# Weight stream of an S5/GLU/MLP/attention trunk on one core: loads strictly in order of use, the GLU with a third raw buffer, the residual in four loads, the GLU's last k-tiles by token halves, and the first MLP splits queued

## The chip, the cores and the metric

The kernel runs on one core of one Trainium2 chip. The time is the device time of one execution in microseconds (us). The kernel before takes 2044.38 us in the median of 3 runs (2044.13 to 2048.23). The engines are named as the profile names them: PE is TensorE's matmuls, PEld its weight loads, DVE is VectorE, ACT is ScalarE, POOL is GpSimd, SP is SyncE, which issues most DMAs. A q behind a name is the queue of DMA issues and semaphores of that engine.

## The reference

A residual stream `h` of 256 tokens by 2048 features, in fp32, passes through four sub-layers, each with an RMS norm ahead and a residual sum behind. `w_glu_a` and `w_glu_b` are 2048x2048, `w_up` and `w_down` 2048x8192 and back.

```python
def sqrelu_mlp(h, w_up, w_down):
    return jnp.square(jax.nn.relu(h @ w_up)) @ w_down

def s5_mixer(u, ...):          # diagonal complex state space, both directions
    ...
    y = y + d_skip.astype(f32) * uf
    z = jax.nn.gelu(y).astype(u.dtype)
    return (z @ w_glu_a) * jax.nn.sigmoid(z @ w_glu_b)

for i in range(DEPTH):         # DEPTH = 2
    if i % N_MIXERS == 0:
        h = h + s5_mixer(rms_norm(h, s5_norm[j]), ...)
    else:
        h = h + windowed_gqa(rms_norm(h, attn_norm[j]), ...)
    h = h + sqrelu_mlp(rms_norm(h, mlp_norm[i]), mlp_w_up[i], mlp_w_down[i])
```

So the order is S5 with its gated unit (GLU), MLP, windowed attention (32 query heads, 4 key heads, softmax with a sink), MLP.

## The kernel before

**Products.** Tokens lie in two halves of 128 (`tt`). Weights come from memory in fp32 and are split on chip into two parts: `hi`, a copy rounded to the type that TensorE multiplies (ScalarE, L682), and `lo`, raw minus `hi` (VectorE, for some tiles GpSimd, L683). Activations are split in the same way. A product is three matmuls, x_hi·w_hi, x_lo·w_hi and x_hi·w_lo (`mm3`, L721 to L723), of 128 by 128 by 512 each. In the MLP's first product the weights are the stationary operand, 16 k-tiles for each of 64 blocks `fb` (L862 for w_hi with both parts of x, L864 for w_lo).

**Weight stream.** All weights go through one list in the order of their use, `self.wsrc`: first 32 GLU tiles of 128x1024, called `wge` here (512 KB each, loaded from ScalarE's queue), then 16 GLU tiles of 128x2048, `wgl` (1 MB, from SyncE's queue, as all that follow), then the MLP's `wup` and `wdn`, attention's `wqkv` and `wo`, and the second MLP. `wload` takes the next entry, asks for a raw, a `hi` and a `lo` buffer from three rings, issues the DMA and writes the split. `wnext` hands over one split tile and keeps one more loaded ahead. An entry's second field says who subtracts: "v" is VectorE, "g" GpSimd; `WP = range(9, 33)` (L36) names the `wge` entries that go to GpSimd (an entry i is the tile i − 1). `wload_fast` (L686) makes the forms for some `wdn` tiles by further subtractions on VectorE.

**Buffers.** For the 1 MB tiles the ring has two raw buffers (19456 and 21504), three for `hi`, three for `lo`. The MLP adds a raw buffer at 49664 and two at 44032 and 46080, which it gives up at block 45; the space at 49664 is free from the end of S5 on.

**Order.** The code is a program for all engines; a scheduler with a model of their times decides the order of instructions on each engine, and with `tc.issue_after(i)` the code can demand that what follows stands behind instruction `i` on its engine. Each engine then runs its list in order. A DMA issue that waits for its buffer holds back what stands behind it on that queue.

**The stages around the change.** The GLU's sums run for four column blocks `cb` of 512 over 16 k-tiles. Its first 8 k-tiles depend on the first half of S5's output and run while S5's second half is computed (`glu_early`, L792, order 1, 2, 3, 0, mixed with S5's expand products on GpSimd, L564 and L565, and its scan on VectorE, L546 to L548; the scan's states are copied at L622 and used by PE at L650). The other 8 run after S5 (`glu_rest`, L835), and beside each block's matmuls the block before is finished by `glu_post` (L811): partial sums added (L820 for the a side, L821 for the b side), sigmoid, product (L826), residual sum (L827), the norm's multiplication by its gain (L739), and four transposes (L748) into the MLP's input, split at L750 and L751. The last block's `glu_post` is handed to `mlp` as `fin`: there the first two MLP blocks run their first 12 k-tiles, with steps of `fin` between them, then the last 4. The residual is loaded whole (2 MB, L1519) from ScalarE's queue before `glu_rest`. Behind the MLP, attention's output tiles `wo` are split while scores (L1224) and softmax (L1239) run head by head.

**The gate.** In `mlp`, the loads asked for at block 6 (`fb == min(SIX)`, L1022) have their splits queued behind `begin`, which are the ScalarE copy and the VectorE addition of the second block's `up_post` (L869).

## Time and profile before

| | us |
|---|---|
| median of 3 runs | 2044.38 |
| the profiled execution's own time | 2044.0 |
| its span in the trace | 2042.2 |
| PE busy in it | 1979.6 |
| DVE busy | 1632.5 |
| ACT busy | 1140.9 |
| POOL busy | 239.5 |

The mean granted TensorE clock of the profiled execution is 0.995 of full speed. Times in the trace run from the span's start. The stages: S5's first half to about 195 us, the early GLU mixed with S5's second half to 286, the late GLU to 389, the change to the MLP to 408, the first MLP to 1066, attention to about 1290, the second MLP to the end. In rows of groups and of the timeline, "out<-in" are the program's names of buffers, "128x2048" is partitions by elements, x is a count, and a bracket at the end of a row of the timeline holds how long the engine was idle before it and what ended that. A row of waits gives the waiting line, what it waited for, the sum in us, how often, and the longest. "slot" is a piece of the large on-chip buffer, "bank" one of the accumulators of TensorE.

### The profile page before, as it was taken

The page shows a single profiled execution, that of the slowest core. Times are in us where ns is not written, and L with a number is a line of the kernel's source. Part 1 is how long each engine was busy: PE and PEld are TensorE (multiplying, and loading weights), DVE is VectorE, ACT ScalarE, POOL GpSimd, SP SyncE. Part 2 cuts the span into 40 slices and gives each one's busy share as a digit, 9 for nine tenths or more (in the row PEclk, how much of TensorE's full clock was granted, in tenths as well). Part 3 has the DMA queues.
Part 4 walks back from the last instruction along what each step waited for, and adds up shares of the span by engine and source line. Part 5 has one row for each costly group of instructions (what it writes and reads, how often), then busy time and mean ns, then how long its engine had stood idle before and what let it go on. Part 6 is the DMA issues. An engine that isn't in the chain of part 4 may idle for free.

```text
span 2042.2 us, 33455 instructions
## 1 busy us (share of the span) xinstructions
PE 1979.6 (97%) x13646; PEld 1671.3 (82%) x13646; DVE 1632.5 (80%) x2474; ACT 1140.9 (56%) x1404; POOL 239.5 (12%) x210
## 2 busy tenths in 40 slices
PE   4989999999999999999999999999999999999999
PEld 4777777788888888888888876888888888888887
DVE  8889736778888888888887877568788888888885
ACT  5553555455555555665554656555555555565553
POOL 6997830000000000000010000000000000000000
PEclk9999999999999999999999999999999999999999
DMA  3234465555555455675555432555555545576554
GB/s 123 68 97 134 145 243 215 181 185 207 206 188 205 165 204 205 232 253 211 214 179 187 147 133 102 218 182 182 180 212 204 205 165 201 204 277 226 201 195 140
DMA packets 62570, 378.99 MB, mean 186 GB/s; under 512 B 7136, under 2 KB 9472, under 8 KB 20944
## 3 DMA queue, kind: packets, MB, share of 16 engines
q1 hardware_dynamic: 55872, 354.90, 48.8%
q10 hardware_dynamic: 5184, 19.49, 2.9%
q0 software_dynamic: 1360, 2.46, 0.6%
q8 instruction: 107, 1.75, 0.3%
q14 instruction: 47, 0.39, 0.1%
HBM read 372.63 MB, written 2.10 MB: 183 GB/s over the span
## 4 chain that ended last, share of the span: by engine, by line
PE 82%; POOL 6%; DVE 5%; ACT 3%; DMA 2%; issue 1%; ACTq 0%; SPq 0%; POOLq 0%; DVEq 0%
PE bank L953 32%; PE bank L862 23%; PE bank L864 12%; PE bank L721 4%; PE bank L723 4%; PE bank L722 4%; POOL slot L564 2%; DVE slot L683 1%; ACT slot L1239 1%; POOL slot L565 1%; POOL slot L505 1%; DMA slot<-in_wge 1%; PE bank L586 1%; PE bank L650 1%; ACT slot L682 1%
## 5 line engine op out<-in xcount | busy, mean ns | idle before, releaser
L683 DVE TENSOR_TENSOR slot<-slot,slot 128x2048 fp32r<-128x2048 f32 (+1 forms) x277 | 597.4, 2161 | 229.5 <-ACT slot L682 222.6
L682 ACT CAST slot<-slot 128x2048 fp32r<-128x2048 f32 (+1 forms) x301 | 519.7, 1734 | 373.5 <-PE bank L953 96.7
L953 PE MATMUL bank<-slot,slot 128*128 128x512 f32 x2532 | 591.3, 390 | 0.0
L953 PEld LDWEIGHTS bank<-slot,slot 128*128 128x128 f32 x2532 | 472.0, 188 | 95.8
L862 PE MATMUL bank<-slot,slot 128*128 128x512 f32 x2048 | 492.7, 391 | 0.1
L862 PEld LDWEIGHTS bank<-slot,slot 128*128 128x128 f32 x2048 | 380.3, 189 | 75.9 <-DVE ms L759 0.3
L698 DVE TENSOR_TENSOR slot<-slot,slot 128x2048 fp32r<-128x2048 f32 (+2 forms) x132 | 241.2, 1827 | 41.1 <-ACT slot L697 40.3
L864 PEld LDWEIGHTS bank<-slot,slot 128*128 128x128 f32 x2048 | 263.1, 191 | 10.3
L864 PE MATMUL bank<-slot,slot 128*128 128x256 f32 x2048 | 266.3, 283 | 0.0
L697 ACT CAST slot<-slot 128x2048 fp32r<-128x2048 f32 (+2 forms) x132 | 203.2, 1540 | 65.8 <-DVE slot L702 48.1
L721 PE MATMUL bank<-slot,slot 128*128 128x512 f32 x544 | 217.1, 400 | 6.1 <-ACT slot L1264 3.1
L722 PE MATMUL bank<-slot,slot 128*128 128x512 f32 x544 | 213.7, 393 | 0.0
L723 PE MATMUL bank<-slot,slot 128*128 128x512 f32 x544 | 207.8, 395 | 4.7 <-POOL slot L683 4.3
L920 ACT CAST slot<-slot 128x512 fp32r<-128x512 f32 (+2 forms) x188 | 108.1, 593 | 58.2 <-PE bank L953 37.3
L721 PEld LDWEIGHTS bank<-slot,slot 128*128 128x128 f32 x544 | 102.7, 189 | 30.9 <-ACT slot L682 3.7
L723 PEld LDWEIGHTS bank<-slot,slot 128*128 128x128 f32 x544 | 102.1, 189 | 28.5 <-POOL slot L683 5.2
L722 PEld LDWEIGHTS bank<-slot,slot 128*128 128x128 f32 x544 | 102.8, 189 | 21.1 <-issue 1.2
L921 DVE TENSOR_TENSOR slot<-slot,slot 128x512 fp32r<-128x512 f32 (+2 forms) x188 | 118.6, 655 | 0.8 <-ACT slot L920 0.8
L869 ACT COPY slot<-bank 128x256 f32<-128x256 f32 x128 | 47.4, 370 | 121.3 <-PE bank L864 120.7
L994 POOL DMA_DIRECT2D slot<-slot x2 | 1.8, 894 | 899.4 <-ACT slot L993 899.4
L872 ACT ACTIVATE slot<-slot 128x256 f32<-128x256 f32 x128 | 53.1, 416 | 68.8 <-DVE slot L870 68.4
L1149 POOL DMA_DIRECT2D slot<-in_pos x1 | 0.8, 784 | 738.7 <-DVE slot L921 738.7
(243 smaller groups left out, 1896.9 us busy)
## 6 DMA issues: line engine op xcount, KB each, us to landing
slot<-in_wup SPq DMA_DIRECT2D x128, 1024.0 KB, 4.9
slot<-in_wdn SPq DMA_DIRECT2D x128, 1024.0 KB, 5.0
slot<-in_wqkv SPq DMA_DIRECT2D x20, 1024.0 KB, 4.9
slot<-in_wge ACTq DMA_DIRECT2D x32, 512.0 KB, 3.8
slot<-in_wgl SPq DMA_DIRECT2D x16, 1024.0 KB, 5.0
slot<-in_wo SPq DMA_DIRECT2D x16, 1024.0 KB, 4.9
slot<-in_wp SPq DMA_DIRECT2D x12, 1024.0 KB, 5.9
slot<-in_bz SPq DMA_DIRECT2D x16, 336.0 KB, 3.3
```

What stands on the lines that cost most here:

```text
L682: self.nc.scalar.copy(hi[:, c], raw[:, c])
L683: (self.nc.gpsimd if e == "g" else self.nc.vector).tensor_sub(lo[:, c], raw[:, c], hi[:, c].bitcast(F32))
L697: self.nc.scalar.copy(hi, x)
L698: v.tensor_sub(lo, x, hi.bitcast(F32))
L721: pe.matmul(out, lhsT=xh, rhs=wh, start=first, stop=False)
L722: pe.matmul(out, lhsT=xl, rhs=wh, start=False, stop=False)
L723: self.dm = pe.matmul(out, lhsT=xh, rhs=wl, start=False, stop=last)
L862: pe.matmul(bk, lhsT=wh[:, kt], rhs=act[:, kt].rearrange("p x c -> p (x c)"), start=(kt == 0), stop=False)
L864: pe.matmul(bk[:, :L], lhsT=wl[:, kt], rhs=act[:, kt, 0], start=False, stop=(kt == KT - 1))
L920: nc.scalar.copy(o[0], h)
L921: v.tensor_sub(o[1], h, o[0].bitcast(F32))
L953: pe.matmul(bank(bk), lhsT=a[x][:, j], rhs=w[y][:, c], start=bk not in begun, stop=stop and y == 1)
```

## The change

1. A new `fetch` issues every 128x2048 weight load from SyncE's queue behind the one before it, in the order of the list. Before, the scheduler could let one pass another.
2. `WP` begins at 12: the `wge` tiles 8, 9 and 10 have their `lo` made by VectorE and not by GpSimd.
3. The raw buffer at 49664 (`self.raw3`) joins the ring in `glu_rest` behind the first k-tile of block 0, and at the second MLP at its beginning; before, the MLP added it after its first two blocks.
4. The residual is loaded in four pieces of 512 KB, one per `cb`, each behind the last weight cast on ScalarE at that point.
5. In the last `cb`, the last four k-tiles run by token halves (`glu_tail`): 24 matmuls for the first half of the tokens and then 24 for the second. Before, each k-tile ran both halves.
6. In `mlp` the splits of the loads asked for at blocks 2 to 11 are queued behind `begin`; before, only those of block 6.

```diff
-WP = range(9, 33)
+WP = range(12, 33)
...
+    def fetch(self, raw, src):
+        with ExitStack() as order:
+            if self.last is not None:
+                order.enter_context(self.tc.issue_after(self.last.ins))
+            self.last = self.nc.sync.dma_start(raw, src)
...
             raw, hi, lo = (r.next() for r in self.wr)
-            (self.nc.scalar if raw.shape[1] < D else self.nc.sync).dma_start(raw, src)
+            if raw.shape[1] < D:
+                self.nc.scalar.dma_start(raw, src)
+            else:
+                self.fetch(raw, src)
...
-                self.nc.scalar.copy(hi[:, c], raw[:, c])
+                self.cast = self.nc.scalar.copy(hi[:, c], raw[:, c])
...
         raw = self.wr[0].next()
-        self.nc.sync.dma_start(raw, src)
+        self.fetch(raw, src)
...
+    def glu_tail(self, bk, kts):
+        w = []
+        for _ in kts[::2]:
+            w.append([t.rearrange("p (n x c) -> p n x c", n=2, x=2) for t in self.wnext()])
+        for tt in range(2):
+            for i, kt in enumerate(kts):
+                wh, wl = w[i // 2]
+                xh, xl = (self.zk(kt)[:, j, tt * P:(tt + 1) * P] for j in range(2))
+                for x in range(2):
+                    self.mm3(bk[tt][x], xh, xl, wh[:, i % 2, x], wl[:, i % 2, x], False, kt == KT - 1)
             yield
...
-            mm = self.glu_mm(bk, range(8, KT)) if cb else self.mm0
+            mm = self.glu_mm(bk, range(8, KT)) if 0 < cb < 3 else self.mm0
+            if cb == 3:
+                mm = chain(self.glu_mm(bk, range(8, KT - 4), range(8, KT)), self.glu_tail(bk, range(KT - 4, KT)))
+            next(mm)
+            cs = slice(cb * 512, (cb + 1) * 512)
+            with self.tc.issue_after(self.cast.ins):
+                self.nc.scalar.dma_start(self.resid[:, :, cs], self.d["xt"][:, :, cs])
             if post is None:
+                self.raw3 = self.ar.get("wx#49664", [2048], at=49664)
+                self.wr[0].add(self.raw3)
                 drain(mm)
             else:
-                next(mm)
                 interleave(mm, (post, 0.7))
...
+        if self.raw3 is None:
+            self.raw3 = ar.get("wx#49664", [2048], at=49664)
+            self.wr[0].add(self.raw3)
...
-        raw3, raw45 = extra(49664), [extra(at) for at in (44032, 46080)]
-        wraw.add(raw3, *raw45)
+        raw45 = [extra(at) for at in (44032, 46080)]
+        wraw.add(*raw45)
...
-                if fb == min(SIX):
+                if fb < 12:
                     for m in begin:
                         gate.enter_context(self.tc.issue_after(m.ins))
...
-                    wraw.drop(raw3, raw4)
+                    wraw.drop(self.raw3, raw4)
+                    self.raw3 = None
...
-        nc.scalar.dma_start(self.resid, d["xt"])
```

How the order of instructions moves is shown at three places. Line numbers of the changed kernel differ: L683 is L693 there, L678 is L674 for SyncE's loads, L732 L742, L739 L749, L751 L761, L820 and L821 L843 and L844, L826 and L827 L849 and L850, L1224 L1258, L1244 L1278, L1240 and L1241 L1274 and L1275.

The first place is SyncE's queue where the GLU's `wgl` tiles begin. slot_83 is the pair of raw buffers, slot_84 the area of the one at 49664, slot_4752 that of the two at 44032 and 46080, and `in_gains` the norm's gain. Before:

```order
L678 DMA slot_83<-in_wgl 128x2048
L678 DMA slot_84<-in_wup 128x2048
L678 DMA slot_83<-in_wgl 128x2048
L732 DMA slot_77<-in_gains 128x512 x2
L678 DMA slot_4752<-in_wup 128x2048 x2
L678 DMA slot_83<-in_wgl 128x2048 x7
```

The same place in the changed kernel:

```order
L674 DMA slot_83<-in_wgl 128x2048 x2
L742 DMA slot_77<-in_gains 128x512 x2
L674 DMA slot_83<-in_wgl 128x2048
L674 DMA slot_84<-in_wgl 128x2048
L674 DMA slot_83<-in_wgl 128x2048 x2
L674 DMA slot_84<-in_wgl 128x2048
```

Three `wup` loads stood among the GLU's tiles; now none does, and the area of slot_84 takes GLU tiles in turn. The `wup` loads begin behind the last `wgl`.

The second place is VectorE at the end of the GLU's last column block. slot_314 holds the partial sums, slot_77 and slot_73 rows of one token half, slot_4068 and slot_4067 the MLP's input. Before:

```order
L821 TENSOR_TENSOR slot_314<-slot_314,bank 128x512
L751 TENSOR_TENSOR slot_4068<-bank,slot_4068 128x4x128
L820 TENSOR_TENSOR slot_314<-slot_314,bank 128x512
L821 TENSOR_TENSOR slot_314<-slot_314,bank 128x512
L820 TENSOR_TENSOR slot_314<-slot_314,bank 128x512
L683 TENSOR_TENSOR slot_3761<-slot_4752,slot_3761 128x2048
L683 TENSOR_TENSOR slot_2734<-slot_83,slot_4070 128x1024
L826 TENSOR_TENSOR slot_77<-slot_314,slot_77 128x512
L683 TENSOR_TENSOR slot_2735<-slot_83,slot_4070 128x1024
L827 TENSOR_TENSOR slot_73<-slot_73,slot_77 128x512
L826 TENSOR_TENSOR slot_77<-slot_314,slot_77 128x512
L739 TENSOR_TENSOR slot_77<-slot_73,slot_77 128x512
```

In the changed kernel:

```order
L844 TENSOR_TENSOR slot_314<-slot_314,bank 128x512
L843 TENSOR_TENSOR slot_314<-slot_314,bank 128x512
L693 TENSOR_TENSOR slot_2735<-slot_83,slot_4069 128x1024 x2
L844 TENSOR_TENSOR slot_314<-slot_314,bank 128x512
L693 TENSOR_TENSOR slot_2734<-slot_84,slot_4069 128x1024
L843 TENSOR_TENSOR slot_314<-slot_314,bank 128x512
L849 TENSOR_TENSOR slot_77<-slot_314,slot_77 128x512
L693 TENSOR_TENSOR slot_2734<-slot_84,slot_4069 128x1024
L761 TENSOR_TENSOR slot_4067<-bank,slot_4067 128x4x128 x2
L850 TENSOR_TENSOR slot_73<-slot_73,slot_77 128x512
L849 TENSOR_TENSOR slot_77<-slot_314,slot_77 128x512
L749 TENSOR_TENSOR slot_77<-slot_73,slot_77 128x512
```

The second half's b addition (the second L844) stands ahead of the first half's product (the first L849), as the second L821 stood before; the 128x2048 split is gone from between them, and the two L761 of the column block before stand behind that product.

The third place is VectorE in attention, around a split for a `wo` tile (the one into slot_2734). slot_4752 (slot_4755 in the changed kernel) holds small rows of the query norm and masks, slot_6431 (slot_6434) the scores. Before:

```order
L210 TENSOR_TENSOR rs_t<-rs_t,rs_h 128x8
L212 SCALAR_TENSOR_TENSOR slot_4752<-rs_t,slot_4752 128x8
L1191 TENSOR_SCALAR slot_4752<-slot_4752,rstd 128x8
L683 TENSOR_TENSOR slot_2734<-slot_83,slot_4070 128x2048
L1224 ISA slot_6431,mx<-bank,slot_4752 128x256
```

In the changed kernel this split stands here:

```order
L1274 TENSOR_TENSOR den<-den,es 128x4
L1275 RECIPROCAL den<-den 128x4
L1278 TENSOR_SCALAR slot_6434<-slot_6434,den 128x256 x4
L1299 TENSOR_TENSOR slot_9576<-bank,slot_9576 128x4x128
L693 TENSOR_TENSOR slot_2734<-slot_83,slot_4069 128x2048
L1221 TENSOR_REDUCE hms<-slot_8091 128x8
```

The split moved from ahead of the head group's scores to behind the end of its softmax (and one of the two splits that came before it moved up to the scores). No line of the diff names attention; this is the scheduler's answer to the rest.

More of the change, by code (lines that the diff above doesn't have):

```diff
@@ L2 @@
 from contextlib import ExitStack
+from itertools import chain
 import numpy as np
@@ L774, in zk, with glu_mm @@
         return self.z[kt // 8][:, KQ[kt // 8][(kt % 8) // 2], kt % 2]
-    def glu_mm(self, bk, kts):
+    def glu_mm(self, bk, kts, full=None):
+        full = full or kts
         n = 1
@@ L785, in glu_mm @@
                 for x in range(2):
-                    self.mm3(bk[tt][x], xh, xl, wh[:, i % n, x], wl[:, i % n, x], kt == kts[0], kt == kts[-1])
+                    self.mm3(bk[tt][x], xh, xl, wh[:, i % n, x], wl[:, i % n, x], kt == full[0], kt == full[-1])
+            yield
+    def glu_tail(self, bk, kts):
[8 more added lines that the diff above has]
+                    self.mm3(bk[tt][x], xh, xl, wh[:, i % 2, x], wl[:, i % 2, x], False, kt == KT - 1)
             yield
@@ L1383, in run @@
         nc, d, ar = self.nc, self.d, self.ar
-        self.wq = []
+        self.wq, self.last = [], None
         def mlp(l):
```

## The prediction

> **What bounds the kernel now.** I read the page's totals and chain first, then busy time by stage, then TensorE's waits in the stages where it is not full, and last the timelines around those waits.
>
> ```profile
> span 2042.2 us, 33455 instructions
> PE 1979.6 (97%) x13646; PEld 1671.3 (82%) x13646; DVE 1632.5 (80%) x2474; ACT 1140.9 (56%) x1404; POOL 239.5 (12%) x210
> PE 82%; POOL 6%; DVE 5%; ACT 3%; DMA 2%; issue 1%; ACTq 0%; SPq 0%; POOLq 0%; DVEq 0%
> ```
>
> TensorE is busy for 97% of the span and carries 82% of the chain. The change removes no matmul, so it can only win idle time or a reduced clock. The busy time by stage says where those are (length, busy PE, PEld, DVE, ACT, POOL with counts, granted clock, DMA share, GB/s):
>
> ```profile
> 195.00:209.00 14.00, 9.59 (x164) 7.09 (x163) 12.70 (x39) 4.44 (x7) 12.29 (x10) 0.88 0.44 143
> 286.00:313.00 27.00, 23.71 (x98) 17.64 (x97) 8.06 (x5) 10.21 (x7) 4.75 (x2) 1.00 0.50 199
> 389.00:408.00 19.00, 14.32 (x72) 12.30 (x71) 16.82 (x41) 6.83 (x11) 0.00 (x0) 0.82 0.34 129
> 408.00:1066.00 658.00, 658.00 (x3373) 564.27 (x3372) 552.23 (x629) 381.43 (x407) 6.48 (x9) 1.00 0.57 204
> 1066.00:1198.00 132.00, 129.44 (x685) 103.93 (x685) 102.40 (x291) 75.13 (x130) 2.62 (x4) 1.00 0.47 165
> 1198.00:1270.00 72.00, 67.67 (x408) 50.01 (x409) 57.67 (x227) 43.33 (x103) 0.00 (x0) 0.98 0.30 103
> 1368.00:1811.00 443.00, 443.00 (x2417) 386.08 (x2416) 370.64 (x439) 251.59 (x287) 0.00 (x0) 1.00 0.56 199
> ...
> 204.30:208.50 4.20, 3.67 (x9) 2.73 (x10) 3.79 (x13) 2.92 (x5) 4.20 (x3) 0.59 0.41 125
> 398.60:405.30 6.70, 6.65 (x29) 5.75 (x30) 5.28 (x27) 2.26 (x4) 0.00 (x0) 0.68 0.31 128
> 1265.30:1269.50 4.20, 4.17 (x18) 2.82 (x19) 3.71 (x17) 0.46 (x1) 0.00 (x0) 0.64 0.00 0
> ```
>
> The MLP stages (658 of 658 us, 443 of 443) are full; nothing can be won there. Four places are not: A (195 to 209) idles 14.00 − 9.59 = 4.4 us, B (286 to 313) 3.3, C (389 to 408) 4.7, D (1198 to 1270) 4.3. Behind three of them the clock is lower: at A by (1 − 0.59) × 4.2 = 1.7 us of lost work, at C by 0.32 × 6.7 = 2.1, at D by 0.36 × 4.2 = 1.5. So A costs 6.1, B 3.3, C 6.8, D 5.8: 22.0 us, and that is the most the change can win. TensorE's waits name the causes (waiting line, releaser, us, times, longest), in the order of A, B, C, before D, D:
>
> ```profile
> PE bank L723 <- POOL slot L683: 3.9, 1, 3.9
> ...
> PE bank L721 <- ACT slot L682: 2.5, 3, 1.3
> PE bank L723 <- POOL slot L683: 0.4, 1, 0.4
> ...
> PE bank L748 <- DVE slot L739: 4.7, 1, 4.7
> ...
> PE bank L1220 <- ACT slot L1211: 1.8, 1, 1.8
> ...
> PE bank L721 <- ACT slot L1264: 3.1, 1, 3.1
> ```
>
> **The change part by part.** The sum is made against the profiled execution's own 2044.0 us (its span 2042.2 and 1.8 around it); the median of the runs, 2044.38, is 0.4 above.
>
> A: three subtractions go from GpSimd to VectorE. TensorE's wait ends with the first of them, queued on GpSimd between S5 products:
>
> ```profile
> 201.94 2.34 POOL L683 TENSOR_TENSOR slot<-slot,slot 128x1024 fp32r<-128x1024 f32 x1
> 204.25 1.10 POOL L564 TENSOR_TENSOR slot<-slot 128x512 f32<-128x512 f32 x1
> ...
> L683 DVE TENSOR_TENSOR slot<-slot,slot 128x1024 fp32r<-128x1024 f32 x8 | 14.5, 1821 | 0.0
> ...
> 395.57 1.22 DVE L683 TENSOR_TENSOR slot<-slot,slot 128x1024 fp32r<-128x1024 f32 x1
> ...
> 235.75 5.67 DVE L622 COPY slot<-slot 64x504 f32<-64x504 f32 x4
> ...
> 246.86 0.22 PE L650 MATMUL bank<-slot,slot 128*64 128x64 f32 x1
> ```
>
> The wait and its clock, 6.1 us, go. In their place VectorE, which is full here with the S5 scan, gets 3 × 1.82 = 5.5 us (the mean beside a busy GpSimd; 3 × 1.22 = 3.7 without it), so the scan's result is 5.5 later while TensorE is 6.1 earlier: 11.6 us closer. The first copy of the scan's states ends at 235.75 + 5.67/4 = 237.2, and TensorE uses it at 246.86: 9.7 us of cover. 11.6 − 9.7 = 1.9 us of new wait, so A gains 4.2. If the subtractions cost 1.22 it gains 6.0; if each waits out a GpSimd product of the longer kind first (2.34 + 1.22 = 3.6, 10.7 in all) the new wait is 16.8 − 9.7 = 7.1 and A loses 1.0. I take 1.82 because it was measured with these neighbours.
> [...] The trace's 1.82 against 1.22 agrees that there is a wait, but not with one of a whole product each time.
>
> B: weight loads in order, a third raw buffer, the residual in four loads. The queues of SyncE and ScalarE, the wait on a load, and the landings between 255 and 312 us:
>
> ```profile
> 256.67 0.37 SPq L678 DMA_DIRECT2D slot<-in_wup  x1
> ...
> 296.61 0.80 SPq L678 DMA_DIRECT2D slot<-in_wup  x2
> 299.23 0.33 SPq L678 DMA_DIRECT2D slot<-in_wgl  x1
> ...
> 275.06 0.36 ACTq L1519 DMA_DIRECT2D slot<-in_xt  x1
> 278.26 0.33 ACTq L678 DMA_DIRECT2D slot<-in_wge  x1
> ...
> 289.02 1.04 ACT L682 CAST slot<-slot 128x1024 fp32r<-128x1024 f32 x1 [2.33 <-DMA slot<-in_wge]
> ...
> slot<-in_xt ACTq DMA_DIRECT2D x1, 2048.0 KB, 11.6
> ```
>
> Three weight tiles of the MLP are loaded before they are of use, two of them 2.6 us ahead of the GLU tile that TensorE needs next, and the residual's 2 MB (11.6 us) stand ahead of a gate tile that was issued at 278.26 and let ScalarE wait until 289.02, 10.7 us later. All of this is behind the needed tiles afterwards, and the third buffer lets one more run ahead, so I take the whole 3.3 us (2.5 if only the waits on ScalarE go). The four residual loads cost ScalarE three more issues of 0.36 us, which lie in its idle time (10.21 busy of 27); each must land before its column block's residual sum, seven k-steps of 12 matmuls later (7 × 12 × 0.227 = 19 us, the 0.227 from C's rows below), against a landing of 11.6/4 = 2.9. Zero; without that cover 2.9 us each.
>
> C: the last four k-tiles by token halves. TensorE's and VectorE's rows there:
>
> ```profile
> 389.66 2.88 PE L862 MATMUL bank<-slot,slot 128*128 128x512 f32 x12
> 392.38 1.59 PE L864 MATMUL bank<-slot,slot 128*128 128x256 f32 x12
> ...
> 398.65 1.11 PE L748 MATMUL bank<-ident,slot 128*128 128x128 f32 x4 [4.68 <-DVE slot L739]
> ...
> 397.91 0.69 DVE L739 TENSOR_TENSOR slot<-slot,slot 128x512 f32<-128x512 f32 x1
> ```
>
> Now the first half's sums end 24 matmuls earlier. One takes (392.38 − 389.66)/12 = 0.227 us, so 24 take 5.4. Call T the first half's end. TensorE then has 5.4 of the second half, the transposes of the block before (0.8 from the 1.11 row, estimated at full clock) and the 12 k-steps of the first MLP block (393.97 − 389.66 = 4.3): it is ready at T + 10.5. VectorE's new order puts the second half's first addition, which needs T + 5.4, ahead of the first half's product. From there to the first half's scaled result it runs eight 128x512 operations of 0.69 and two subtractions of 1.22: 5.4 + 5.5 + 2.4 = T + 13.3. A wait of 2.8 is left of 4.7, and I leave half of the lost clock, 1.0. C gains 6.8 − 3.8 = 3.0, from 0 (the same wait by way of the addition) to 6.8.
> A wait of 1.8 us (before D) was followed by a clock of 1.00, one of 3.1 (at D) by 0.64, so 2.8 is undecided by rows. [...]
>
> D: attention. No edit is there, but the order that follows from the new loads differs from 1198 us on. Before, VectorE holds a split for a weight tile that has not landed, and the scores stand behind it:
>
> ```profile
> 1220.39 2.29 DVE L683 TENSOR_TENSOR slot<-slot,slot 128x2048 fp32r<-128x2048 f32 x1 [3.54 <-ACT slot L682]
> ```
>
> Now that split stands behind the softmax, which starts 3.5 + 2.3 = 5.8 us earlier. The last wait of TensorE in this stage is for the end of such a chain (3.1, and 1.5 of clock). I take these 4.6 as won; the ends are 5.8 (all of D) and −2.3 (the split, later, becomes the late one).
>
> The queue in the MLP: the splits of the loads asked for in blocks 2 to 11 stand behind the second block's ScalarE copy and VectorE addition. The first MLP is full to the last tenth from 408 on, and a block lasts 4.3 × 16/12 = 5.7 us of TensorE. A queued split needs a cast and a subtraction:
>
> ```profile
> L683 DVE TENSOR_TENSOR slot<-slot,slot 128x2048 fp32r<-128x2048 f32 (+1 forms) x277 | 597.4, 2161 | 229.5 <-ACT slot L682 222.6
> L682 ACT CAST slot<-slot 128x2048 fp32r<-128x2048 f32 (+1 forms) x301 | 519.7, 1734 | 373.5 <-PE bank L953 96.7
> ...
> slot<-in_wup SPq DMA_DIRECT2D x128, 1024.0 KB, 4.9
> ```
>
> 1.73 + 2.16 = 3.9 us, inside the block of 5.7 ahead of it: zero. Uncovered, it costs these 3.9 once.
>
> Sum: 4.2 + 3.3 + 3.0 + 4.6 = 15.1 us; 2044.0 − 15.1 = 2028.9, say 2029.
>
> **The rivals.** 0.2% is 4.1 us, about what a measurement of this kernel can tell from no change.
> First, D stays: the new order only moves the wait to another product. For it: no edit touches attention. The gain is 10.5, the time 2033.5.
> Second, A turns round: the scan is late by the long figure, a wait of 7.1 appears at TensorE's use of its states, with 1.7 of clock behind it as at A. A loses 2.7 instead of gaining 4.2: 2044.0 − 8.2 = 2036. For it: VectorE is busy 12.70 of 14.00 there. Against: the measured 1.82.
> Third, the waits are hidden replacements: B's tiles wait for a buffer rather than for a load, C's addition waits as before, D stays, and A gives 2 or so: 2042, no change. Against: B's rows name a DMA and C's a VectorE queue.
> Fourth, slower: strict order on SyncE starves the MLP. A load whose buffer is not free now holds back every load behind it, where before another could pass. With the three buffers that are left after block 45, a tile holds a buffer for 4.9 + 1.73 + 2.16 = 8.8 us, so one can start each 2.9 us, against a TensorE block of 5.7: this speaks against it. It needs VectorE or ScalarE to be late by a block. At 0.6 us for each of the 36 late blocks in both MLPs it loses 22 against the 15.1 won: 2044.0 + 7 = 2051; it decides from 15.1/36 = 0.4 us a block.
>
> **How the numbers follow.** My case of all four places 0.45, D stays 0.2, A turns round 0.13, no change 0.1, starved 0.08; 0.04 is left for small mixtures around no change and slower. Faster by over 0.2% holds the first three: 0.78; same 0.13; slower 0.09. The time is the likeliest case's 2029; its own range is 2024 to 2036 from the ends of A and C. The low end takes all 22.0 us: 2022. The high end reaches past the second rival to nearly no change, 2041, which leaves out the fourth rival and most of the third.
>
> **What would show it.** A: no wait of TensorE on GpSimd at 200 us, granted clock 1.00, and a wait below 3 us at the use of the scan's states. B: SyncE issues no MLP tile before the last GLU tile, ScalarE's casts never wait over 2 us for a gate tile, and TensorE is full from 280 to 310. C: the wait ahead of the first half's transposes is 2 to 3 us. D: no idle VectorE ahead of the split, and no wait over 1 us at the stage's end. The MLPs keep a full TensorE; idle time there, with SyncE's loads issued late, would be the fourth rival. A stall longer than 4 us at the scan's states would make A wrong, and unchanged waits at D with all else right would put the time at 2033.5.

## The result, and the profile after

The changed kernel takes 2027.87 us in the median of 6 runs (2026.83 to 2029.61), the kernel before 2044.26 (2041.77 to 2048.23, 6 runs): a ratio of 0.992, with a 95% interval of 0.9909 to 0.993. That is 16.4 us faster, where 15.1 and 2029 were forecast. The profiled execution has a span of 2025.8 us. Its page's totals and its chain:

```profile
span 2025.8 us, 33472 instructions
PE 1974.2 (97%) x13646; PEld 1669.6 (82%) x13646; DVE 1635.6 (81%) x2477; ACT 1140.0 (56%) x1404; POOL 236.1 (12%) x207
PE 87%; DVE 6%; POOL 4%; ACT 1%; issue 1%; DMA 1%; ACTq 0%; SPq 0%; POOLq 0%; DVEq 0%
```

The matmuls are as many as before, and TensorE's share of the chain rose from 82 to 87%. The same stretches as in the prediction, by the clock of the new trace:

```profile
195.00:209.00 14.00, 12.83 (x184) 10.01 (x184) 13.14 (x32) 3.94 (x6) 11.68 (x10) 1.00 0.51 174
286.00:313.00 27.00, 27.00 (x120) 22.28 (x120) 12.74 (x6) 12.65 (x7) 2.93 (x2) 1.00 0.61 229
389.00:408.00 19.00, 19.00 (x113) 16.77 (x112) 12.87 (x35) 9.94 (x13) 0.00 (x0) 1.00 0.33 125
408.00:1066.00 658.00, 658.00 (x3359) 563.87 (x3358) 556.10 (x631) 381.31 (x408) 6.52 (x9) 1.00 0.58 208
1198.00:1270.00 72.00, 69.99 (x440) 53.20 (x440) 57.20 (x205) 47.95 (x107) 0.00 (x0) 1.00 0.33 114
1368.00:1811.00 443.00, 443.00 (x2395) 385.26 (x2394) 370.20 (x433) 254.61 (x286) 0.00 (x0) 1.00 0.56 199
```

The granted clock is 1.00 in all of them, the stretch of B went from 98 to 120 matmuls, and both MLPs are full as before. TensorE's waits that are left, at A, at C, ahead of D and at D:

```profile
PE bank L587 <- ACT slot L605: 1.3, 1, 1.3
PE bank L731 <- ACT slot L825: 1.1, 1, 1.1
PE bank L733 <- POOL slot L693: 0.7, 1, 0.7
...
PE bank L895 <- DVE slot L761: 2.0, 1, 2.0
...
PE bank L1254 <- ACT slot L1245: 1.9, 1, 1.9
...
PE bank L731 <- ACT slot L1298: 2.0, 1, 2.0
```

Stretches of two traces at the same microseconds do not hold the same work. So the comparison goes by the work done: both traces hold all 768 matmuls of the GLU's products ahead of the first MLP block, and I compare the starts of the same one. A runs from the first to the 265th of them, B from there to the 721st, C to the third MLP block's first matmul, D over all of attention. Each entry is the stage's length less that of before. "Start" is S5 ahead of the GLU, which no edit touches; its −3.0 to 1.1 is what one execution differs from another by. Behind the bar stands the clock that was lost, the sum of (1 − granted clock) × 5 us over the stage in steps of 5 us. It counts time in which TensorE waits too: of the 3.5 at C before, 2.1 fell on work (0.32 × 6.7, as in the prediction). One execution each:

```
kernel       start     A     B     C  MLP1     D  MLP2 | clock lost: A    B    C    D
before           0     0     0     0     0     0     0 |           1.7    0  3.5  1.8
changed       -0.2  -1.7  -5.1  -4.6  -0.1  -4.9  -0.1 |             0    0    0    0
u_wp           1.1   0.1  -5.1  -3.3   0.2  -1.2  -0.1 |           1.7    0  1.7  3.4
u_order       -0.3  -1.6  -0.7  -4.8   0.2  -3.3  -0.1 |             0  1.7    0  1.7
u_resid       -1.8  -1.7  -1.5  -3.3   0.2  -3.1  -0.1 |             0    0  1.7  1.7
u_raw3         0.2  -1.4  -4.8  -2.7   0.0  -4.5  -0.1 |             0    0  1.7  1.7
u_tail        -2.0  -1.7  -4.9  -5.3   0.2  -2.3  -0.1 |             0    0    0  1.7
o_gate        -3.0   0.5   0.6  -5.3   0.2  -4.5  -0.1 |           3.4    0    0    0
u_gate        -0.9  -1.4  -5.1  -0.6  -0.7  -2.1  -0.1 |             0    0  1.8    0
t_gate        -2.5  -1.4  -5.1   0.9  -0.1  -6.7  -0.1 |             0    0  3.4    0
tail_r1       -1.7  -2.0  -5.1  -7.1   0.2   0.0  -0.1 |             0    0    0  1.7
f1            -1.5  -1.8  -5.1  -0.6  -0.7  -0.2  -0.1 |             0    0  1.7  1.7
tr_f1          0.4  -1.3  -5.1  -7.1   0.2   3.2  -0.1 |             0    0    0  5.1
tail_split    -2.8  -1.4  -5.1  -7.1   0.2  -4.2  -0.1 |             0    0    0    0
```

The 16.4 us come from A 1.7, B 5.1, C 4.6 and D 4.9, and nothing from the MLPs. The times of all runs follow with each experiment; the stages above are repeatable to some tenths wherever the order is the same and the clock lost is the same (see B in eight rows).

### The profile page after: what moved, and what is told of

It is laid out like the page before. It is cut to its first block, busy times and chain, and to the rows that moved or that the text cites. A ratio compares the mean times of both kernels' runs of the same rounds, so it can differ in the third digit from the quotient of the medians.

```text
span 2025.8 us, 33472 instructions
## 1 busy us (share of the span) xinstructions
PE 1974.2 (97%) x13646; PEld 1669.6 (82%) x13646; DVE 1635.6 (81%) x2477; ACT 1140.0 (56%) x1404; POOL 236.1 (12%) x207
## 4 chain that ended last, share of the span: by engine, by line
PE 87%; DVE 6%; POOL 4%; ACT 1%; issue 1%; DMA 1%; ACTq 0%; SPq 0%; POOLq 0%; DVEq 0%
PE bank L986 32%; PE bank L895 23%; PE bank L897 12%; PE bank L731 5%; PE bank L733 5%; PE bank L732 5%; DVE slot L693 1%; POOL slot L565 1%; POOL slot L506 1%; ACT slot L1273 1%; POOL slot L566 1%; DVE bank L547 1%; PE bank L1293 1%; PE bank L1284 1%; PE bank L651 0%
## 5 line engine op out<-in xcount | busy, mean ns | idle before, releaser
L693 DVE TENSOR_TENSOR slot<-slot,slot 128x2048 fp32r<-128x2048 f32 (+1 forms) x280 | 601.2, 2152 | 213.6 <-ACT slot L692 201.1
L732 PE MATMUL bank<-slot,slot 128*128 128x512 f32 x544 | 213.1, 392 | 0.0
L732 PEld LDWEIGHTS bank<-slot,slot 128*128 128x128 f32 x544 | 102.3, 188 | 20.5 <-issue 0.5
L986 PE MATMUL bank<-slot 128*128 128x512 f32 x342 | 82.6, 389 | 0.0
```

Source lines behind the costliest of these rows:

```text
L693: (self.nc.gpsimd if e == "g" else self.nc.vector).tensor_sub(lo[:, c], raw[:, c], hi[:, c].bitcast(F32))
L732: pe.matmul(out, lhsT=xl, rhs=wh, start=False, stop=False)
L986: pe.matmul(bank(bk), lhsT=a[x][:, j], rhs=w[y][:, c], start=bk not in begun, stop=stop and y == 1)
```

## The experiments

Medians and ratios are against the kernel before in the same set of runs. In the names, u stands for one part of the change undone.

**u_wp: A by itself.**

```diff
-WP = range(12, 33)
+WP = range(9, 33)
```

> The changed kernel with WP = range(9, 33) again, so that three subtractions go back to GpSimd. By the two traces, the place A (195 to 286 us) is worth 1.7 us net: 4.8 us are won by matmul 120 of the GLU and 2.9 are given back by matmul 264. The scheduler's order in attention also goes back to that of before (both splits ahead of the scores), and with it D's 4.9 us. My theory: 2027.9 + 1.7 + 4.9 = 2034.5, with the loss split so between the two places. Rival 1 (the prediction's size of A, 4.2): 2037. Rival 2 (D does not hang on the order of the split): 2029.6, with attention as fast as in the changed kernel.

2034.51 us, ratio 0.9953 (0.9938 to 0.9968). At A the wait on GpSimd is back at full length:

```profile
PE bank L733 <- POOL slot L693: 4.0, 1, 4.0
PE bank L731 <- ACT slot L825: 0.5, 1, 0.5
```

A loses all of its gain, 1.8 us and no more: rival 1, my own size of 4.2, falls. B does not change. In attention the split stands ahead of the scores again, though the order around it is not that of before: some 160 of the 1456 instructions in TensorE's list stand elsewhere. The stage is 3.7 slower than in the changed kernel, of which 3.4 is clock; so this run alone does not say what the order is worth, and that the time is the expected 2034.5 is partly luck.

**u_order and u_resid: B's two loads.** In the first the forced order goes, in the second the residual is one load of 2 MB again.

```diff
-            if self.last is not None:
-                order.enter_context(self.tc.issue_after(self.last.ins))
```

> The changed kernel without the forced order of SyncE's loads: two MLP weight tiles go again ahead of the third pair of GLU tiles, with the third raw buffer kept; attention's order is that of the changed kernel. My theory: the loads ahead of their turn cost part of what B won (5.1 us between matmuls 336 and 456 of the GLU), about half: 2030.5, all of it between those matmuls. Rival 1 (the third buffer and the residual in four loads are the whole of B): 2027.9. Rival 2 (strict order costs the MLP, so that its absence wins there): below 2027.

2032.35 us, ratio 0.9939 (0.9922 to 0.9956).

```diff
+        nc.scalar.dma_start(self.resid, d["xt"])
...
-            with self.tc.issue_after(self.cast.ins):
-                self.nc.scalar.dma_start(self.resid[:, :, cs], self.d["xt"][:, :, cs])
```

> The changed kernel with the residual in one load of 2 MB ahead of the late GLU, as before; everything else and attention's order as in the changed kernel. My theory: the 2 MB stand ahead of a gate tile, which lands later, and about half of B's 5.1 us is lost between matmuls 336 and 456: 2030.5. Rival (the MLP tiles ahead of their turn were the whole cause, and 2 MB on the other queue is hidden): 2027.9.

2031.13 us, ratio 0.9936 (0.9921 to 0.9951). First SyncE's queue in u_order, then ScalarE's in u_resid, then TensorE's wait between 280 and 320 us in the one and in the other:

```profile
292.84 0.80 SPq L672 DMA_DIRECT2D slot<-in_wup  x2
294.32 23.62 SPq L672 DMA_DIRECT2D slot<-in_wgl  x6
...
271.56 0.36 ACTq L1550 DMA_DIRECT2D slot<-in_xt  x1
...
286.16 1.05 ACT L692 CAST slot<-slot 128x1024 fp32r<-128x1024 f32 x1 [2.97 <-DMA slot<-in_wge]
...
PE bank L729 <- ACT slot L690: 2.4, 1, 2.4
...
PE bank L731 <- ACT slot L692: 1.8, 2, 1.5
```

Two `wup` tiles 1.5 us ahead of the GLU tile cost 4.4 of B's 5.1 us (a wait of 2.4 and 1.7 of clock behind it; 0.3 is open). The 2 MB cost 3.6. Both rivals fall; the parts do not add: each alone loses most of B's 5.1, and their sum is 8.0. That the MLP wins without the strict order falls too: in u_order MLP1 is 0.2 and MLP2 −0.1.

**u_raw3: the third buffer.** The buffer joins at the beginning of the MLP only.

```diff
-                self.raw3 = self.ar.get("wx#49664", [2048], at=49664)
-                self.wr[0].add(self.raw3)
+                self.raw3 = None
                 drain(mm)
```

> The changed kernel with the third raw buffer only from the MLP's beginning on. A tile holds a raw buffer for 5.0 us of load, 1.7 of cast and 2.2 of subtraction, 8.9 in all, and feeds 24 matmuls of 0.2275, 5.5 us: two buffers give a tile each 4.4 us, which is enough. My theory: in order, the third buffer adds nothing but a few tenths: 2027.9 to 2029, attention's order being that of the changed kernel (1.7 more if the clock falls there). Rival (the buffer is what B needs at the change from the small tiles to the large): 2 to 4 us lost between matmuls 336 and 456: 2030 to 2032.

2029.28 us, ratio 0.9926 (0.9911 to 0.9941). B is −4.8 and the waits of TensorE from 280 to 320 us are none. The buffer is worth 0.3 us there; most of the rest of the difference to the changed kernel in this execution is the clock, lost once at C and once in attention.

**u_tail: C without the token halves.**

```diff
-            mm = self.glu_mm(bk, range(8, KT)) if 0 < cb < 3 else self.mm0
-            if cb == 3:
-                mm = chain(self.glu_mm(bk, range(8, KT - 4), range(8, KT)), self.glu_tail(bk, range(KT - 4, KT)))
+            mm = self.glu_mm(bk, range(8, KT)) if cb else self.mm0
```

> The changed kernel with the last four k-tiles of the GLU in the old order, both token halves together. My theory: C's 4.6 us are lost between the GLU's matmul 744 and the third MLP block; the scheduler's order in attention goes back to that of before at the same time, and D's 4.9 with it: 2037.4. Rival 1 (C was won by the 128x2048 split that no longer stands between the last block's additions, and not by the halves): 2033 to 2034, with C as in the changed kernel. Rival 2 (D does not hang on the order): 2032.5.

2028.23 us, ratio 0.9923 (0.9908 to 0.9938): the changed kernel's time. TensorE's waits at the end of the GLU, in u_tail and (again) in the changed kernel:

```profile
PE bank L758 <- DVE slot L749: 1.5, 1, 1.5
...
386.56 1.19 PE L895 MATMUL bank<-slot,slot 128*128 128x512 f32 x4 [2.05 <-DVE slot L761]
```

My theory falls: C is −5.3 without the halves and −4.6 with them. The halves only change the wait. With them, the eight transposes of the block before come behind the GLU, the split of their result (L761) stands late on VectorE, and k-tiles 8 to 11 of the first MLP block wait for it. Rival 1 holds as to C: something else made it. Its time does not, since attention lost 2.6 and not 4.9.

**o_gate, u_gate and t_gate: the queued splits.** o_gate is the kernel before with the gate alone, u_gate the changed kernel with the old gate, t_gate the same without the halves too.

```diff
-                if fb == min(SIX):
+                if fb < 12:
```

> The kernel before with the last part of the change alone: the splits of the loads asked for at blocks 2 to 11 queued behind begin. The two splits (2.29 + 1.22 us) leave VectorE's list ahead of the last column block's norm, so by my present theory TensorE's wait there falls from 4.7 to about 1.3 us and with it part of the 3.5 us of lost clock: C wins 4 to 6 of what the changed kernel wins there, without the token halves. Attention gets another order, worth 1 to 5 us more: 2035 to 2039. Rival 1 (the token halves are what shortens C): the wait stays at 4.7, and only attention can change: 2040 to 2044. Rival 2 (the queued splits are late for the first MLP's blocks): a new wait within 25 us of the third MLP block, slower than the kernel before.

2033.81 us, ratio 0.9951 (0.9936 to 0.9966).

> The changed kernel with the gate at block 6 alone, as before, and with the token halves. VectorE's list has the same order up to the last norm multiplication; the split of an MLP tile comes only behind it. My theory: halves and gate do the same thing, each alone is enough, so C stays within 1.7 us (one event of the clock) of the changed kernel; attention has the order of before and loses 2 to 4: 2030 to 2033. Rival (the gate alone is the cause of C): C loses 3.5 us of splits and up to 3.5 of clock: 2034 to 2037.

2033.54 us, ratio 0.9946 (0.9931 to 0.9961).

> The changed kernel without the token halves and without the new gate: only loads in order, third buffer, residual in four and the three subtractions are left. My theory: two splits stand among the last block's operations on VectorE again, TensorE waits about 5 us (1.5 + 3.5) for the norm, the clock goes, and C is lost whole: 4.6 to 5.3 against the changed kernel; with attention's third order another 0 to 4: 2033 to 2037. Rival (C came from the GLU's loads being in order, whatever stands on VectorE): 2028 to 2031.

2029.66 us, ratio 0.9928 (0.9911 to 0.9944). TensorE's waits at C in o_gate, u_gate and t_gate, in this order:

```profile
PE bank L748 <- DVE slot L739: 1.5, 1, 1.5
...
PE bank L895 <- DVE slot L761: 3.6, 2, 2.1
...
PE bank L758 <- DVE slot L749: 5.5, 1, 5.5
```

The gate alone takes the wait from 4.7 to 1.5 and C to −5.3, as expected: the gain at C belongs to the edit that I had put at zero. In u_gate the rival of my theory holds, the halves do not cover for the gate: without it three splits on VectorE (1.22, 2.28 and 1.22 us) stand between the last norm multiplication and the last L761, and TensorE waits twice (2.05 and 1.51). Without both, the wait is 5.5 and C is 0.9 worse than before, as my theory had it; that t_gate's time falls into the rival's range is luck, by attention's −6.7.

**tail_r1: the halves placed so that they can pay.**

```diff
-                interleave(mm, (post, 0.7))
+                interleave(mm, (post, 0.7 if cb < 3 else 1.0))
```

> The changed kernel with the steps of the block before handed out at a rate of 1.0 and not 0.7 in the last column block, where the token halves leave fewer steps of the main loop. Its eight transposes then come before the GLU's end, and the splits that the first MLP block's k-tiles 8 to 11 need leave their place behind the norm on VectorE. My theory: TensorE's wait of 2.05 us on those splits goes, the first half's norm is ready at about T + 5.5 where TensorE comes at T + 9.8, so no wait takes its place: C wins 1.5 to 2 against the changed kernel. Attention falls back to the order of before, which costs 1 to 3: 2026.5 to 2029.5, between matmul 720 and the third block 6.0 to 6.6 us less than before. Rival (the halves are worth nothing however they are placed): a wait of 1.5 as in the kernel without halves, C no better than there.

2030.42 us, ratio 0.9937 (0.9924 to 0.9951). C is −7.1, 2.5 better than in the changed kernel. TensorE goes through the change of stage without a wait:

```profile
380.77 2.88 PE L895 MATMUL bank<-slot,slot 128*128 128x512 f32 x12
383.49 1.60 PE L897 MATMUL bank<-slot,slot 128*128 128x256 f32 x12
384.92 0.60 PE L758 MATMUL bank<-ident,slot 128*128 128x128 f32 x4
385.28 3.00 PE L895 MATMUL bank<-slot,slot 128*128 128x512 f32 x12
```

The rival falls: the halves are worth 1.8 against u_tail once the transposes are out of their way. But attention fell back to before's order and to before's time, 4.9 slower than in the changed kernel, 1.7 of it clock, where 1 to 3 were expected; the whole is no better than the changed kernel.

**f1, tr_f1 and tail_split: attention's order by itself.** All three force the cast and the subtraction of one `wo` tile behind a softmax: in f1 (on u_gate) and tr_f1 (on tail_r1) behind the last one written before it, which puts it behind the next head group's scores; in tail_split (on tail_r1) behind the softmax of the very group whose scores it stood ahead of, where the changed kernel has it. The lines are those of tail_split; f1 and tr_f1 go over `self.soft`, the last softmax, and an "s" marks the tile.

```diff
-                self.cast = self.nc.scalar.copy(hi[:, c], raw[:, c])
...
+                with ExitStack() as behind:
+                    for m in self.softs[2, 0, 1] if e == "s" else ():
+                        behind.enter_context(self.tc.issue_after(m.ins))
+                    self.cast = self.nc.scalar.copy(hi[:, c], raw[:, c])
```

> The changed kernel with the old gate (u_gate, 2033.5), and in attention one wo tile's cast and subtraction forced behind the softmax of the head group whose scores they stood ahead of; up to there the order is that of u_gate. My theory: the split ahead of the scores is what D loses, so attention wins 2.5 to 3 against u_gate (2.1 us ahead of before there, with the clock at 1.00): about 5 ahead of before, 2030.5 to 2031.5. Rival (what differed between the kernels in attention was only the clock, which falls in some executions by 1.7, and not the order): no change against u_gate within 1, 2032.5 to 2034.5.

2035.35 us, ratio 0.9964 (0.9952 to 0.9977).

> Both together: the changed kernel with the steps of the block before at a rate of 1.0 in the last column block, and the same wo tile's split forced behind the softmax. My theory: the gains add, 1.5 to 2 at C against the changed kernel, and attention as in the changed kernel or better: 2025 to 2027. Rival (each only moves the wait to the next product): 2027.5 to 2029.5, as the changed kernel or tail_r1.

2031.39 us, ratio 0.9943 (0.993 to 0.9955).

> The kernel with the steps of the block before at a rate of 1.0 in the last column block (tail_r1, which won 7.1 us at C and nothing in attention), and the third wo split of the earlier runs put where the changed kernel has it: right behind the softmax of the head group whose scores it stood ahead of, and ahead of the next group's scores, not one group later as in f1 and tr_f1. My theory: it is this place that made attention faster in the changed kernel, by 3 to 5 us against before, so the gains at C and in attention add: 2024.5 to 2027 with the clock at 1.00 in attention, 1.7 more if it falls once. Rival (the place of the split does not matter, attention's gain in the changed kernel came from the other splits of that order or from the clock alone): attention at 0 to 2 against before, 2028 to 2030.5, as tail_r1.

2026.2 us, ratio 0.9919 (0.9905 to 0.9933). TensorE's waits from 1200 to 1300 us in f1, tail_r1 and tail_split:

```profile
PE bank L734 <- ACT slot L1302: 2.3, 1, 2.3
PE bank L736 <- DVE slot L696: 2.1, 1, 2.1
PE bank L1288 <- DVE slot L1281: 1.8, 1, 1.8
...
PE bank L731 <- ACT slot L1298: 3.1, 1, 3.1
PE bank L1254 <- ACT slot L1245: 0.8, 1, 0.8
...
PE bank L1298 <- ACT slot L1291: 1.7, 1, 1.7
PE bank L1257 <- ACT slot L1248: 1.2, 1, 1.2
```

f1 and tr_f1 went against me: one group later, the split is itself what TensorE waits for (L696, 2.1), and attention is 1.9 and 3.2 us slower than in u_gate and tail_r1, 1.7 and 3.4 of it clock: the waits in sum did not get shorter. At its exact place it pays: D goes from 0.0 to −4.2 between tail_r1 and tail_split, 1.7 of it the clock that did not fall. Of the other 2.5, TensorE's waits over all of attention explain 0.8 (6.9 us in sum, then 6.1); the rest is open. Nor does the split move alone: the scheduler answers the one forced place with another order, in which some 170 of the 1456 instructions in TensorE's list stand elsewhere. So the pair shows that the order of attention is worth these 2.5 us, and not that this one place is. tail_split has the fastest profiled execution of all (a span of 2022.0), but its ratio's interval overlaps that of the changed kernel (0.9909 to 0.993), so it is not shown to be faster.

## Why the prediction was right, and where its steps were off

The direction, the size and the four places were right: 15.1 forecast, 16.4 measured, the MLPs at zero. None of the four terms was right by its whole working: A was 2.5 too high, B 1.8 and C 1.6 too low, and D came near in size though the wait that it took as gone stayed. That the errors made up for each other is luck. Three signs that I had named did not show: ScalarE still waited 3.9 us for a gate tile (at 283, where TensorE did not feel it), C's wait was not ahead of the transposes, and at the end of D a wait of 2.0 was left where at most 1 was allowed.

**A, forecast 4.2, measured 1.7.** The wait and its clock went as said: from the 97th to the 121st matmul of the GLU the changed kernel wins 6.0 us (6.1 forecast). What failed is the step that puts a wait for the scan's states, and nothing else, in the wait's place. That wait (1.9 forecast) did not come. TensorE has no idle time there: the first copy of the states ends at 239.02 + 6.56/4 = 240.7, and they are used from 245.79. Between matmuls 217 and 265, with the same work in both traces, the changed kernel does lose 0.7, but TensorE is busy throughout; it changes 16 times between the GLU's matmuls and S5's where it changed 12 times; whether that is the cause was not shown. Two waits came that I had not named. One of 1.1 is for ScalarE's copies of partial sums (L825) ahead of the place, and 1.2 are lost there. The other is for GpSimd: TensorE is now 6 us early, and at 210.8 its next S5 products (L587) are held by a copy that itself waits for a GpSimd product, and at 214.7 a matmul by the first subtraction left on GpSimd. This pair gives back 2.4, so that 6.0 − 1.2 − 2.4 − 0.7 = 1.7 is left:

```profile
209.00 1.10 POOL L565 TENSOR_TENSOR slot<-slot,slot 128x512 f32<-128x512 f32 x1
...
210.13 0.59 ACT L605 COPY slot<-bank 128x512 f32<-128x512 f32 x1 [7.13 <-POOL slot L565]
...
214.66 0.51 PE L733 MATMUL bank<-slot,slot 128*128 128x512 f32 x1 [0.68 <-POOL slot L693]
...
239.02 6.56 DVE L623 COPY slot<-slot 64x504 f32<-64x504 f32 x4
...
245.79 0.34 PE L651 MATMUL bank<-slot,slot 128*64 128x64 f32 x4
```

I had asked what is late next on VectorE alone, and not on the engine that the work was taken from. GpSimd was itself slowed: two of the moved subtractions cost its products 1.9 us (last section). Without these the product at 209.00 would have ended at 208.2, ahead of TensorE's need; this is an estimate, which no run tried.

**B, forecast 3.3, measured 5.1.** The mechanism was right, and u_order and u_resid show both of its loads to be causes; the size was read from the wrong column. 27.00 − 23.71 is idle time, but a matmul after a wait counts as busy for some 0.5 us (0.50 behind the waits of 0.82 and 0.36 at 290.12 and 296.94 before, 0.51 in the row at 214.66 above), where in C's rows before, without a wait, one follows the other at 0.227. The counts in the same rows say more: 98 matmuls in 27 us against 120, and 22 × 0.227 = 5.0.

**C, forecast 3.0, measured 4.6.** A near number for the wrong edit. I gave the gain to the token halves and zero to the queue of splits; o_gate has −5.3 from the queue alone, and the halves, as placed here, cost 0.7. (Without the queue they win 1.5 between t_gate and u_gate, as much as the difference in lost clock.) The step that failed is the count on VectorE's list: the difference that mattered was the two splits (2.29 and 1.22) that the queue takes from it in o_gate, and I counted eight operations and two other splits from T on without asking which edit had removed the rest. The wait of 2.8 that I left was measured as 2.05, but on another instruction: k-tiles 8 to 11 of the block that I used as cover read the transposes of the block before, whose split I had myself placed late on VectorE.

**D, forecast 4.6, measured 4.9.** The scores after the split start at 1205.76 where they started at 1222.60:

```profile
1222.60 0.42 DVE L1224 CUSTOM_DVE_ANT_0 slot<-bank,slot 128x256 f32<-128x256 f32 x1
...
1205.76 0.42 DVE L1258 CUSTOM_DVE_ANT_0 slot<-bank,slot 128x256 f32<-128x256 f32 x1
```

Of the 16.8 us between them 11.7 were won ahead of attention; 5.1 are won up to these scores, against 5.8 forecast. The step that failed comes behind them: I took the whole wait at the stage's end as won, 3.1, and it is still 2.0. Over all of attention TensorE's waits fall from 6.8 to 5.0 us in sum and the lost clock from 1.8 to 0; 1.3 of the 4.9 are neither, and their cause is open. What the forecast overstated is how sure the clock is: 1.8 of the 4.9 is clock that by luck did not fall in this execution (last section), while u_order and u_resid with the same order and the same last wait of 2.0 lost 1.7. So the near size is in part luck. That the order makes D is shown by tail_r1, whose attention has before's order and before's time, and by tail_split; that the one split's place makes it is not. u_wp and u_tail keep it ahead of the scores and win 1.2 and 2.3 all the same, with 3.4 and 1.7 of lost clock; their order around it is another than before's.

**The rivals.** Starved MLPs by strict order: not seen, TensorE is full in both. The first rival, D stays, is what before's order gives (0.0 in tail_r1), and not what the changed kernel got. A turned round: its wait at the scan's states did not come at all. No change: it falls with the gains at B, C and D. Open stays why t_gate's attention, in yet another order, is fastest of all (−6.7); its order was not tried by itself.

## What to carry to other kernels

Compare two traces by the n-th piece of the same work, and read a lost stretch from the count of matmuls in it rather than from the busy share. When a wait is taken away, look for the next late input on every engine, the relieved one too, and ask whether the moved work and what stays behind can run at the same time; and look on a list of instructions for what has vanished from it, not only for what was moved. A scheduler answers an edit far from it (attention here, 800 us later), so the order of the whole program belongs to the change, and an experiment that undoes one part is read stage by stage.

## What the runs showed of the hardware that I had not expected

**The clock fell behind one wait of 2 us and not behind another.** At C the changed kernel and u_resid have the same wait of 2.05 us ahead of the same matmul. Ten microseconds around it, in the changed kernel and in u_resid:

```profile
381.60:391.60 10.00, 7.95 (x47) 6.69 (x46) 9.94 (x29) 4.61 (x9) 0.00 (x0) 1.00 0.94 374
...
384.50:394.50 10.00, 7.95 (x38) 6.61 (x37) 8.52 (x21) 3.89 (x9) 0.00 (x0) 0.83 0.95 394
```

The first kept a clock of 1.00, the second lost 0.17 × 10 = 1.7 us. In the table the loss comes in portions of 1.7 or 1.8, 3.4 or 3.5, and 5.1.

What differs between the two can be read from the traces. In the trace of the kernel before the clock falls three times from 150 us to the end of attention, at 204.89, 396.04 and 1266.44 us, for 3.41, 6.83 and 3.41 us, each time to 0.50; the starts lie 56 and 255 times 3.413 us apart. These are steps of that length around the same wait, two of the changed kernel and then two of u_resid (length, busy PE, and the granted clock third from the end):

```profile
381.85:385.26 3.41, 2.66 (x16) 1.98 (x14) 3.41 (x5) 2.40 (x4) 0.00 (x0) 1.00 0.85 295
385.26:388.68 3.42, 2.12 (x14) 1.95 (x15) 3.42 (x7) 0.72 (x2) 0.00 (x0) 1.00 1.03 431
...
385.20:388.61 3.41, 1.40 (x7) 0.80 (x5) 3.41 (x6) 1.15 (x3) 0.00 (x0) 1.00 0.95 399
388.61:392.02 3.41, 3.37 (x11) 2.98 (x12) 3.35 (x10) 1.45 (x4) 0.00 (x0) 0.50 1.01 425
```

In the changed kernel a border between two steps cuts the wait into 0.75 and 1.30 us, and the clock stays at 1.00. In u_resid 2.01 us lie in one step, and the next step has a clock of 0.50. At D the changed kernel's last wait of 2.0 lies with 0.52 us in one step and 1.49 in the next, and the clock stays at 1.00; behind the last wait of 2.0 in u_order 1.7 us of clock were lost (0.17 × 10 from 1254.30 to 1264.30). The steps around the falls of the kernel before, and last the step with the longest idle time of TensorE in the changed kernel from 150 us to the end of attention:

```profile
201.48:204.89 3.41, 0.50 (x1) 0.19 (x1) 3.10 (x10) 0.20 (x1) 3.41 (x3) 1.00 0.18 71
204.89:208.31 3.42, 2.98 (x7) 2.40 (x8) 3.11 (x10) 2.53 (x5) 3.42 (x3) 0.50 0.51 153
392.63:396.04 3.41, 1.34 (x12) 1.14 (x10) 3.41 (x4) 0.58 (x2) 0.00 (x0) 1.00 0.32 67
396.04:399.45 3.41, 0.80 (x5) 0.80 (x5) 3.26 (x6) 1.00 (x3) 0.00 (x0) 0.50 0.96 401
399.45:402.87 3.42, 3.42 (x10) 2.74 (x9) 3.42 (x20) 1.21 (x3) 0.00 (x0) 0.50 0.36 149
1263.03:1266.44 3.41, 1.11 (x7) 0.77 (x9) 2.46 (x11) 2.73 (x9) 0.00 (x0) 1.00 0.00 0
1266.44:1269.85 3.41, 3.41 (x16) 2.35 (x13) 2.92 (x14) 0.35 (x1) 0.00 (x0) 0.50 0.00 0
...
1177.15:1180.57 3.42, 1.75 (x8) 1.12 (x6) 2.14 (x10) 3.42 (x13) 0.00 (x0) 1.00 0.00 0
1180.57:1183.98 3.41, 3.02 (x24) 2.32 (x24) 3.41 (x10) 3.41 (x6) 0.00 (x0) 1.00 0.00 0
```

Idle times of 2.91, 2.07, 2.61 and 2.30 us in one step were each followed by a step at 0.50, and the 1.67 in the changed kernel by one at 1.00. So a wait of 2.05 us cost itself in one trace, and itself and 1.7 in another. That its place among these steps decides between the two fits these rows; no run moved a wait to test it. The runs of the changed kernel spread from 2026.83 us at a mean clock of 0.999 to 2029.61 at 0.995; only one of them has a trace.

**Subtractions on VectorE and products on GpSimd ended one behind the other.** The three subtractions that moved, and the GpSimd products beside two of them:

```profile
197.38 1.22 DVE L693 TENSOR_TENSOR slot<-slot,slot 128x1024 fp32r<-128x1024 f32 x1
...
200.16 1.61 DVE L693 TENSOR_TENSOR slot<-slot,slot 128x1024 fp32r<-128x1024 f32 x1
...
202.68 1.33 DVE L693 TENSOR_TENSOR slot<-slot,slot 128x1024 fp32r<-128x1024 f32 x1
...
198.52 2.17 POOL L565 TENSOR_TENSOR slot<-slot,slot 128x512 f32<-128x512 f32 x2 [1.85 <-DMA slot<-in_cp]
...
200.65 2.28 POOL L566 TENSOR_TENSOR slot<-slot,slot 128x512 f32<-128x512 f32 x1
203.01 1.97 POOL L565 TENSOR_TENSOR slot<-slot 128x512 f32<-128x512 f32 x1
```

They took 4.2 us together where 5.5 were forecast, and the products 2.28 and 1.97 us where the same lines take some 1.28 and 1.11 elsewhere in this trace: GpSimd lost 1.9 us. The ends show how. The second product in the row at 198.52 ends at 200.69, and the subtraction issued meanwhile ends 1.08 us later, at 201.77, where one without a product beside it takes 1.22. The product that starts at 200.65 ends 1.16 after that, and the last subtraction again 1.08 after the product. In the traces of both kernels it is so for all 18 subtractions of this size that began while such a product was in flight (8 before, 10 in the changed kernel, all between 166 and 205 us): each ends 1.08 us after the product in flight, and the next product 0.96 to 1.16 after the subtraction. So the times fit a subtraction and a product that wait for what is left of each other's instruction and then take nearly their own time (1.08 beside 1.22, 0.96 to 1.16 beside 1.10 to 1.30); for other instructions no run shows it. The prediction's 3.6 each was too high, because it let every subtraction wait out a whole instruction of GpSimd; the three took 0.0, 0.4 and 0.1 us more than 1.22.
